# The second layer's first phase as three staggered streams, and the context's recurrence beside the attention

## The chip, the cores and the metric

One core of one Trainium2 chip runs the whole program: TensorE (PE; its weight loads are shown as PEld), VectorE (DVE), ScalarE (ACT), GpSimd (POOL) and SyncE (SP), which issues most of the DMAs. The metric is device time in microseconds for one execution.

## The reference, cut to what matters

Two transformer blocks run one after the other; the first has two layers. The change is in the second of these layers, whose mixer joins a neighbourhood attention to an RWKV-7 recurrence. The recurrence runs in both directions, first over the 256 context tokens from a zero state, then over the 512 latent tokens from the state that the context left:

```python
def odd_mixer(h, hc, ...):
    q, k, v, zd = _split(h @ w_in, (C_W, C_W, C_W, D_SHIFT_W))
    qc, kc, vc, zdc = _split(hc @ w_in, (C_W, C_W, C_W, D_SHIFT_W))
    y_c = neighborhood_attention(heads(q, C_HEADS), heads(k, C_HEADS), heads(v, C_HEADS), kc, vc, rpb)
    lat = rwkv7_inputs(centred_shift_mix(zd, mu), ...)
    cx = rwkv7_inputs(centred_shift_mix(zdc, mu), ...)
    s_fwd, yc_fwd = wkv7_scan(zero, cx, 0, False, need_ctx)
    s_bwd, yc_bwd = wkv7_scan(zero, cx, 1, True, need_ctx)
    _, y_fwd = wkv7_scan(s_fwd, lat, 0, False, True)
    _, y_bwd = wkv7_scan(s_bwd, lat, 1, True, True)
    y_d = rwkv7_readout(y_fwd + y_bwd, lat, r_k, ln_w, ln_b)
    y = jnp.concatenate([y_c, y_d], axis=-1) @ w_out

def step(S, inp):                      # of wkv7_scan
    w_t, k_t, v_t, kk_t, a_t = inp[:5]
    sa = jnp.einsum('bhvk,bhk->bhv', S, kk_t)
    S = (S * w_t[:, :, None, :] - sa[..., None] * (kk_t * a_t)[:, :, None, :]
         + v_t[..., None] * k_t[:, :, None, :])
    return S, (jnp.einsum('bhvk,bhk->bhv', S, inp[5]) if emit else None)
```

There are eight heads of 64 channels. All arithmetic is float32.

## The kernel before

The recurrence is worked in chunks of 64 tokens, and two heads (a pair, `j` from 0 to 3) share the 128 partitions. "c" names the context's stream (4 chunks), "l" the latents' (8 chunks). For each stream the work is cut into three parts.

Phase 1 (`rw_phase1`, `rw_pair`, `rw_dir`) makes everything that doesn't need the state. `mix` makes one projection of 128 channels: 24 matmuls into a PSUM tile `psz`, a shift by POOL (`ms`, L869) and two steps on DVE (L870, L871). There are nine of them in the context's stream and fourteen in the latents'. For each pair and direction `d`, `rw_dir` makes gates and decays from two small products (`psw`, `psa`), a scan and two exponentials on ACT, scales the operands (`az`, `BKn`), multiplies them chunk by chunk into the PSUM tile `psA` (L1004), masks these into `M` on DVE (L1006), makes a second product from `M` and the values (L1011) and stores it all in DRAM. `az` holds the two heads of a pair apart by zeros, so that one product of 128 rows gives both heads, side by side. The tiles `t1` to `t3` exist once for each direction.

`rw_tri` loads the small triangular blocks (`Al`) and solves them on DVE: 31 steps of a product into PSUM (`Tl`, L792) and a subtraction (`Zl`, L794), for both directions, interleaved by the scheduler with whatever else DVE has to do. Its results go to the DRAM images `dZ` and `dZT` (L1041), direction 0 by SP's queue and direction 1 by ACT's. Context and latents use the same images.

`rw_phase2` is the recurrence proper: units (`rw_unit`) of one block of two chunks, one direction and two pairs; 8 units for the context and 16 for the latents. A unit loads its operands, makes a chain of products (`p1`, `p2`, `pb`, `pt`, `p3`: L1070 to L1096, all in PSUM tiles of one pool) with a copy or subtraction by ACT or DVE behind each, and then steps twice through the state `G` (`psc`, L1114 and L1123, with `UV`, L1116, and the update of `G`, L1126). `fl` says how many units are open at once: one for the context, three for the latents.

In program order the layer runs thus: the context's phase 1 with the attention's key and value projections (`na_proj`, PSUM tiles `psn`) between its steps; the latents' phase 1 with the context's solve and the context's recurrence between its steps; the attention (`na_attn`, 32 units of a 128-query block and a head) with the latents' solve between its steps; the latents' recurrence; the readout. Work named `side` is advanced by `step` at each `yield` of the main work. Tiles are allotted in this program order, and each engine then executes its own queue strictly in the order that the scheduler left.

Of the kernel before, what the change touches and what calls it, by code (L numbers as in the profile page):

```python
# [766 lines left out]
class K1:  # L767
# [74 lines left out]
    def rw_phase1(self, s):  # L842
# [4 lines left out]
        with ExitStack() as es:  # L847
# [6 lines left out]
            s.ops = {}  # L854
            s.az = [pi.tile([128, s.nar, 2, n], F32, name=f"az{i}") for i in range(2)]
            s.vu = [pi.tile([128, s.nch, 128], F32, name=f"vu{i}") for i in range(2)]
            for z in s.az + s.vu:
                nc.gpsimd.memset(z, 0.0)
# [3 lines left out]
            def mix(w, cidx, dst):  # L862
# [10 lines left out]
            def mixes(j, gap=1):  # L873
                out = []
                for i, tag in enumerate("kvr" if s.lat else "kv"):
                    out.append(tp.tile([128, n], F32, tag=tag, name=tag))
                    mix(self.wget(("1d", 1 + 4 * i + j)), 1 + 4 * i + j, out[-1])
                    for _ in range(gap):
                        yield
                kvr[j] = out  # L880

            kvr = {}
            mix(self.wget(("1d", 0)), 0, s.tw)
            yield
            nc.scalar.activation(s.tw[0:64], s.tw[0:64], AF.Tanh)
            def gate():
                yield
                mix(self.wget(("1d", 13)), 13, self.gsig)
                nc.scalar.activation(self.gsig, self.gsig, AF.Sigmoid)

            yield from mixes(0)
            self.rw_pair(s, 0, pi, tp, *kvr[0])
            for j in range(4):
                gens = [self.rw_dir(s, d, j, tp) for d in range(2)]
                if j < 3:
                    gens.append(self.chained(mixes(j + 1, 2 if s.lat else 1), lambda: self.rw_pair(s, j + 1, pi, tp, *kvr[j + 1])))
                elif s.lat:
                    gens.append(gate())
                op = s.ops[j]
                while gens:  # L900
                    for g in list(gens):
                        if next(g, self) is self:
                            gens.remove(g)
                    yield
                if s.lat:
                    self.rw_bonus(s, j, op)

    def chained(self, gen, last):
        yield from gen
        last()  # L910

    def rw_pair(self, s, j, pi, tp, k, v, r=None):

        nc = self.nc
        n = s.n
        lora = pi.tile([128, 4, 128], F32, tag="lora", name="lora", bufs=2)
        nc.sync.dma_start(lora, self.ap["lora"][:, :2048].rearrange("p (a b c) -> p a b c", a=4, b=4)[:, :, j])
        kk = tp.tile([128, n], F32, tag="kk", name="kk")
        vu = s.vu[j % len(s.vu)]
        s.ops[j] = (lora, k, v, r, kk, vu, {})  # L920
# [8 lines left out]
        nc.vector.tensor_tensor(kk, kk, sq, op=ALU.mult)  # L929
        pt = s.psd("pvt")  # L930
# [4 lines left out]
        nc.sync.dma_start(s.dV[:, j], vu[64:128])  # L935

# [11 lines left out]
    def rw_dir(self, s, d, j, tp):  # L948
# [3 lines left out]
        lora, k, v, r, kk, vu, kds = s.ops[j]  # L952
# [30 lines left out]
        for e in range(2):  # L983
            p = slice(64 * e, 64 * e + 64)
            if s.lat:
# [9 lines left out]
        w = nar * 128  # L995
        per = 512 // w
        mk = self.b(f"mar{d}")[:, :w].unsqueeze(1).to_broadcast([128, per, w])
        hc = max(per, nch // 2)
        for g in range(0, nch, per):
            if g % hc == 0:  # L1000
                M = tp.tile([128, hc, nar, 2, 64], F32, tag=f"M{d}", name="M", bufs=1)
# [4 lines left out]
            nc.vector.tensor_tensor(M[:, g % hc:g % hc + per].rearrange("p c s e t -> p c (s e t)"), ps.rearrange("p (c x) -> p c x", c=per), mk, op=ALU.mult)  # L1006
            yield
            for c in range(g, g + per):
                for e in range(2):
                    o = ((c - g) // 2) * 128 + e * 64  # L1010
                    nc.tensor.matmul(ps[64 * (c % 2):64 * (c % 2) + 64, o:o + 64], M[:, c % hc, 0, e], vu[:, c, e * 64:e * 64 + 64], start=True, stop=True)  # L1011
            nc.scalar.activation(t2[:, g * 64:(g + per) * 64], ps[:, :per * 64], AF.Copy)
            if (g + per) % hc == 0:
                g0 = g + per - hc
                for c in range(2):
                    nc.sync.dma_start(s.dA[d][:, c, g0 // 2:(g0 + hc) // 2, j].rearrange("p b e t -> p b (e t)"), M[0:64, c::2, 0].rearrange("p b e t -> p b (e t)"))
                if s.lat:
                    nc.sync.dma_start(s.dRR[d][:, j, g0:g0 + hc], M[:, :, 1].rearrange("p c e t -> p c (e t)"))
# [312 lines left out]
    def layer1(self):  # L1331
# [48 lines left out]
        for _ in na:  # L1380
            next(tri, None)
# [835 lines left out]
```

## Time and profile before

| | us |
|---|---|
| median of 3 runs | 3802.57 |
| lowest and highest of them | 3797.42, 3802.86 |
| the profiled execution | 3793.68 |
| its span, first to last instruction | 3791.9 |

PE is busy for 3377.0 us (89% of the span), DVE for 1701.5 (45%), POOL for 1402.0 (37%), ACT for 1308.5 (35%). The mean granted clock of TensorE is 0.945 of full speed. These shares are means over stages with different limits. The second layer's mixer lies between about 1134 and 1866 us from the span's start, and in it PE is less busy than elsewhere.

### The profile page before, as it was taken

Reading aid. Unit: us, or ns where it says so; the run is one execution under the profiler, and the core shown is the slowest. Engines: PE = TensorE matmul, PEld = TensorE weight load, DVE = VectorE, ACT = ScalarE, POOL = GpSimd, SP = SyncE. Lnnn points to the kernel's source line nnn. Section 1 sums busy time; section 2 is a strip of 40 time slices with the busy share of each in tenths; the row PEclk is TensorE's granted clock in tenths of the full one; section 3 lists DMA queues with packets and bytes.
Section 4 is the critical chain, followed back from the end, with each engine's and each line's share of the span. In section 5 each row is a group of like instructions: output and inputs, shape, how many; then the busy total and the mean of one; then the engine's idle time right before and its main releaser. Section 6 shows DMA issues by size and latency. Waiting matters only on the chain. (4 is left out here: it accounts for less than half of the span.)

```text
span 3791.9 us, 49466 instructions
## 1 busy us (share of the span) xinstructions
PE 3377.0 (89%) x18772; PEld 2652.6 (70%) x18772; DVE 1701.5 (45%) x3170; ACT 1308.5 (35%) x2263; POOL 1402.0 (37%) x940
## 2 busy tenths in 40 slices
PE   7989989999999768888889989997898698789997
PEld 3679868787878546667768877666777457658885
DVE  4566231111124596574554426447657767431112
ACT  3366231121224433332234432333545323232222
POOL 1453222222223453321335544434544343244442
PEclk9999999999999878999889999998999899999999
DMA  6420243434334434636423433433455668512221
GB/s 230 164 106 7 88 151 117 150 116 141 126 106 129 111 111 140 175 88 204 146 70 124 131 105 95 122 93 99 140 155 155 158 193 247 164 61 95 95 97 65
DMA packets 397757, 480.78 MB, mean 127 GB/s; under 512 B 148432, under 2 KB 288656, under 8 KB 396496
## 3 DMA queue, kind: packets, MB, share of 16 engines
q1 hardware_dynamic: 384976, 476.05, 40.6%
q10 hardware_dynamic: 12544, 1.57, 0.3%
q8 instruction: 149, 2.44, 0.3%
q14 instruction: 88, 0.72, 0.1%
HBM read 391.86 MB, written 85.66 MB: 126 GB/s over the span
## 5 line engine op out<-in xcount | busy, mean ns | idle before, releaser
L322 POOL TENSOR_TENSOR wlo<-wraw,whi 128x1024 fp32r<-128x1024 f32 (+2 forms) x371 | 867.1, 2339 | 1512.7 <-ACT whi L321 1345.3
L321 ACT ACTIVATE whi<-wraw 128x1024 fp32r<-128x1024 f32 (+2 forms) x371 | 380.2, 1026 | 1041.3 <-issue 240.8
L504 DVE TENSOR_TENSOR pu<-pu,sg 128x512 f32<-128x512 f32 x88 | 55.6, 632 | 606.9 <-PE pu L361 554.2
L361 PE MATMUL pd<-hidh,wlo 128*128 128x512 f32 (+1 forms) x704 | 262.0, 372 | 9.2 <-POOL wlo L322 8.9
L361 PE MATMUL pd<-hidh,whi 128*128 128x512 f32 (+1 forms) x704 | 263.4, 374 | 6.1 <-ACT whi L321 3.8
L361 PE MATMUL pd<-hidl,whi 128*128 128x512 f32 (+1 forms) x704 | 260.5, 370 | 0.2 <-DVE hidl L506 0.2
L361 PE MATMUL pg<-hil,whi 128*128 128x512 f32 x528 | 214.3, 406 | 28.8 <-ACT hil L449 15.4
L361 PE MATMUL pg<-hil,wlo 128*128 128x512 f32 x528 | 211.4, 400 | 8.1 <-POOL wlo L322 7.1
L361 PE MATMUL pu<-hil,whi 128*128 128x512 f32 x528 | 209.7, 397 | 5.8 <-ACT whi L321 5.8
L361 PE MATMUL pu<-hil,wlo 128*128 128x512 f32 x528 | 209.2, 396 | 6.0 <-POOL wlo L322 6.0
L361 PE MATMUL pg<-lol,whi 128*128 128x512 f32 x528 | 210.5, 399 | 2.5 <-DVE lol L450 2.4
L361 PE MATMUL pu<-lol,whi 128*128 128x512 f32 x528 | 208.9, 396 | 0.0
L361 PE MATMUL psp<-hil,whi 128*128 128x512 f32 x416 | 174.0, 418 | 25.6 <-DVE yo L1782 11.8
L361 PE MATMUL psp<-lol,whi 128*128 128x512 f32 x416 | 171.0, 411 | 2.9 <-DVE lol L450 2.9
L361 PE MATMUL psp<-hil,wlo 128*128 128x512 f32 x416 | 170.3, 409 | 1.9 <-POOL wlo L322 1.8
L513 DVE SCALAR_TENSOR_TENSOR xT<-pd,mod,xT 128x512 f32<-128x512 f32 x80 | 59.8, 749 | 244.6 <-PE pd L361 244.6
L361 PEld LDWEIGHTS pd<-hidh,whi 128*128 128x128 f32 x704 | 133.3, 189 | 46.8 <-issue 15.1
L361 PEld LDWEIGHTS pd<-hidh,wlo 128*128 128x128 f32 x704 | 133.4, 189 | 39.1 <-POOL wlo L322 15.4
L361 PEld LDWEIGHTS pg<-hil,whi 128*128 128x128 f32 x528 | 101.5, 192 | 71.8 <-ACT hil L449 18.6
L361 PEld LDWEIGHTS pd<-hidl,whi 128*128 128x128 f32 x704 | 133.3, 189 | 24.0 <-issue 0.9
L792 DVE TENSOR_TENSOR Tl<-Al,Zl 64x31 f32<-64x31 f32 (+15 forms) x248 | 145.2, 585 | 4.1
L1574 DVE SCALAR_TENSOR_TENSOR psp<-xpl,vecs,psp 128x512 f32<-128x512 f32 x144 | 107.8, 751 | 84.5 <-ACT psp L1570 58.1
(588 smaller groups left out, 8145.9 us busy)
## 6 DMA issues: line engine op xcount, KB each, us to landing
mraw<-in_wm_dram SPq DMA_DIRECT2D x144, 512.0 KB, 4.3
wraw<-in_w2c_dram SPq DMA_DIRECT2D x72, 512.0 KB, 3.3
wraw<-in_wf0in_dram SPq DMA_DIRECT2D x44, 512.0 KB, 3.6
wraw<-in_wf1in_dram SPq DMA_DIRECT2D x44, 512.0 KB, 3.6
Z<-dZ SPq DMA_DIRECT2D x48, 256.0 KB, 3.8
ZT<-dZT SPq DMA_DIRECT2D x48, 256.0 KB, 4.1
wraw<-in_w1d_dram SPq DMA_DIRECT2D x23, 512.0 KB, 3.9
wraw<-in_wf2g_dram SPq DMA_DIRECT2D x22, 512.0 KB, 3.2
```

Source lines behind the costliest of these rows:

```text
L321: self.nc.scalar.activation(hi[:, :nk], t[:, :nk], AF.Copy)
L322: self.nc.gpsimd.tensor_tensor(lo[:, :nk], t[:, :nk], hi[:, :nk].bitcast(F32), op=ALU.subtract)
L361: nc.tensor.matmul(ps, l, r, start=first and i == 0 and p == 0, stop=last and i == n - 1 and p == 2)
L504: nc.vector.tensor_tensor(u, u, sg[:, :n], op=ALU.mult)
L513: nc.vector.scalar_tensor_tensor(x[:, j], pd[:, :n], gv[:, j:j + 1], x[:, j], op0=ALU.mult, op1=ALU.add)
L792: nc.vector.tensor_tensor(tmp, A[:L, rows, t:t + 1].to_broadcast([L, nr, ncl]), Z[:L, t:t + 1, cols].to_broadcast([L, nr, ncl]), op=ALU.mult)
L1574: nc.vector.scalar_tensor_tensor(pv, xp[:, :, t:t + L], w(t), pv, op0=ALU.mult, op1=ALU.add)
```

## The change

Phase 1 no longer runs the two directions of one pair beside the next pair's projections. Each pair is one stream (`rw_pair`) that makes its own `k`, `v` and `r` and then opens its two directions two steps apart; up to three such streams are open, started six rounds apart (five in the context's). `az` loses its zeros and its second copy: each head's product takes its own 64 rows, into one PSUM tile for each head. The PSUM pool of the latents' phase 1 has five tiles instead of two; the attention's transposes have one instead of two. The projections beside the context's phase 1 advance at every second step. Only the context's solve stays beside the latents' phase 1; the context's recurrence, with one PSUM tile in each of its two pools instead of two, advances twice in each round of the attention. All stores of the solves go by SP's queue.

```diff
-            s.az = [pi.tile([128, s.nar, 2, n], F32, name=f"az{i}") for i in range(2)]
+            s.az = [pi.tile([128, s.nar, n], F32, name=f"az{i}") for i in range(2)]
...
-            yield from mixes(0)
-            self.rw_pair(s, 0, pi, tp, *kvr[0])
-            for j in range(4):
-                gens = [self.rw_dir(s, d, j, tp) for d in range(2)]
-                if j < 3:
-                    gens.append(self.chained(mixes(j + 1, 2 if s.lat else 1), lambda: self.rw_pair(s, j + 1, pi, tp, *kvr[j + 1])))
...
+            yield from self.rounds((self.rw_pair(s, j, pi, tp, mix) for j in range(4)), 3, 6 if s.lat else 5)
...
+        op = (lora, k, v, r, kk, vu, {})
+        for i, _ in enumerate(self.rounds((self.rw_dir(s, d, j, tp, op) for d in range(2)), 2)):
+            if i == 4 and s.lat:
+                self.rw_bonus(s, j, op)
...
-        for e in range(2):
-            p = slice(64 * e, 64 * e + 64)
-            if s.lat:
-                nc.gpsimd.tensor_tensor(ch(az[p, 1, e]), ch(r[p]), E[p, :, i0:i0 + 64], op=ALU.mult)
-                nc.sync.dma_start(s.dR[d][p, j], az[p, 1, e])
-            nc.vector.tensor_tensor(ch(az[p, 0, e]), ch(kk[p]), E[p, :, iprev:iprev + 64], op=ALU.mult)
-            nc.sync.dma_start(s.dAf[d][p, j], az[p, 0, e])
+        if s.lat:
+            nc.gpsimd.tensor_tensor(ch(az[:, 1]), ch(r), E[:, :, i0:i0 + 64], op=ALU.mult)
+            nc.sync.dma_start(s.dR[d][:, j], az[:, 1])
+        nc.vector.tensor_tensor(ch(az[:, 0]), ch(kk), E[:, :, iprev:iprev + 64], op=ALU.mult)
+        nc.sync.dma_start(s.dAf[d][:, j], az[:, 0])
...
-            ps = s.psv("psA")
+            pa = [s.psv("psA") for e in range(2)]
             for c in range(per):
-                nc.tensor.matmul(ps[:, c * w:c * w + w], BKn[:, g + c].rearrange("p s t -> p (s t)"), az[:, :, :, (g + c) * 64:(g + c) * 64 + 64],
-                                 start=True, stop=True)
+                for e in range(2):
+                    p = slice(64 * e, 64 * e + 64)
+                    nc.tensor.matmul(pa[e][:, c * w:c * w + w], BKn[p, g + c].rearrange("p s t -> p (s t)"), az[p, :, (g + c) * 64:(g + c) * 64 + 64],
+                                     start=True, stop=True)
...
-                        (nc.sync, nc.scalar)[d].dma_start(dst[sl, :, sl].rearrange("i u j -> u i j"), z[Lq * p:Lq * p + Lq])
+                        nc.sync.dma_start(dst[sl, :, sl].rearrange("i u j -> u i j"), z[Lq * p:Lq * p + Lq])
...
-            pT = P("npT", 2, space=PSUM, side="right")
+            pT = P("npT", 1, space=PSUM, side="right")
...
-            st_c.side, st_c.bq, st_c.bc, st_c.bl, st_c.bk = "right", 2, 2, 1, 1
+            st_c.side, st_c.bq, st_c.bc, st_c.bl, st_c.bk = "right", 1, 1, 1, 1
...
-            for _ in self.rw_phase1(st_c):
-                self.step()
+            for i, _ in enumerate(self.rw_phase1(st_c)):
+                if i % 2 == 0:
+                    self.step()
...
-        with self.pool(name="psd1c", bufs=2, space=PSUM) as pA, self.pool(name="psd1f", bufs=2, space=PSUM) as pD:
+        with self.pool(name="psd1c", bufs=2, space=PSUM) as pA, self.pool(name="psd1f", bufs=5, space=PSUM) as pD:
...
-            self.side = chain(self.rw_tri(st_c), self.rw_phase2(st_c))
-            for i, _ in enumerate(self.rw_phase1(st_l)):
-                self.step(2 if i > 16 and i % 2 else 1)
+            self.side = self.rw_tri(st_c)
+            for _ in self.rw_phase1(st_l):
+                self.step()
...
-        tri = self.rw_tri(st_l)
+        tri, rec = self.rw_tri(st_l), self.rw_phase2(st_c)
         for _ in na:
             next(tri, None)
+            next(rec, None)
+            next(rec, None)
         run(tri)
+        run(rec)
```

What this makes of the queues shows at the end of the attention. On PE, before, the attention's last transposes and products (`pt`, `po`) are followed by the latents' recurrence (`p` with L1070 and L1076):

```order
L1259 MATMUL ps<-nkz_12786,nq 128x256
L1289 MATMUL po<-ptile,nv 64x128 x8
L1272 MATMUL pt<-consts,p 128x128 x8
L1289 MATMUL po<-ptile,nv 64x128 x8
L1070 MATMUL p_13946<-ZT,U_13923 128x128 x4
L1076 MATMUL p_13952<-Z,V_13951 128x128 x4
L1070 MATMUL p_13977<-ZT,U_13923 128x128 x4
```

In the changed kernel the same place of PE's queue reads as follows (L1258 and L1275 are the attention's transposes and products, L1056 to L1082 a unit's chain, L1100 and L1109 its steps through `G_9342`; the states and `U_12353`, `U_12354` are the context's):

```order
L1275 MATMUL po<-ptile,nv 64x128 x8
L1258 MATMUL pt<-consts,p 128x128 x8
L1275 MATMUL po<-ptile,nv 64x128 x8
L1056 MATMUL p_13013<-ZT,U_12354 128x128 x4
L1062 MATMUL p_13019<-Z,V_13018 128x128 x4
L1068 MATMUL pb<-consts,BK 128x128 x4
L1072 MATMUL pt<-consts,A 128x128 x2
L1079 MATMUL p_13110<-Z_13096,at 64x128 x4
L1082 MATMUL p_13110<-BV,Z_13096 128x64 x4
L1100 MATMUL psc<-G_9342,LU 64x128 x2
L1056 MATMUL p_13221<-ZT,U_12353 128x128 x3
L1109 MATMUL psc<-UV,bk 128x128 x2
```

This is the fourth of the context's eight units. Three of them stand among the attention's products; the other five stand here, behind all of them and ahead of the latents' recurrence, each but for its `p1` and `p2` behind the one before it.

On SP's queue of the changed kernel the stores of the latents' solve (L1027) stand ahead of that fourth unit's loads of `Z` and `ZT` (L1038, L1039), which read the same images; `dno` is the attention's output:

```order
L1224 DMA nv<-dnv_9436 64x384
L315 DMA wraw<-in_w1out_dram 128x1024
L1027 DMA dZ_1507<-Zl 32x32x32 x4
L1027 DMA dZT_1509<-Al 32x32x32 x4
L1027 DMA dZ_1508<-Zl 32x32x32 x4
L1027 DMA dZT_1510<-Al 32x32x32 x4
L1038 DMA Z<-dZ_1508 128x512
L1280 DMA dno_9439<-no 128x512
L1280 DMA dno_9440<-no 128x512
L1039 DMA ZT<-dZT_1510 128x512
```

Sixteen stores now stand in one queue; before, eight stood in SP's and eight in ACT's. So the fourth unit and all later ones can start only when the latents' solve is done and stored.

On DVE's queue of the changed kernel the solve's last step (L792, L794) stands ahead of ten of the attention's 32 row maxima (`nm`, L1247); before, only one maximum stands within the solve's last two steps, and none behind the last. The place in the changed kernel:

```order
L1247 TENSOR_REDUCE nm<-ps 128x1
L792 TENSOR_TENSOR Tl<-Al,Zl 128x31
L1248 TENSOR_SCALAR nm<-nm 128x1
L792 TENSOR_TENSOR Tl<-Al,Zl 128x31
L794 TENSOR_TENSOR Zl<-Zl,Tl 128x31 x2
L1252 RECIPROCAL sm<-sm 128x1
L1247 TENSOR_REDUCE nm<-ps 128x1
L1248 TENSOR_SCALAR nm<-nm 128x1
L1247 TENSOR_REDUCE nm<-ps 128x1
```

What moved is the end of the solve, from the end of the attention to a place with ten units of it to come.

## Rows read from the trace of the kernel before

**Rows 1.** Busy times by stretch: us, engines (instructions), granted clock, DMA share, GB/s

```profile
1134.00:1304.00 170.00, 138.50 (x888) 119.85 (x888) 86.79 (x157) 75.36 (x136) 74.73 (x54) 0.91 0.45 127
1304.00:1577.00 273.00, 210.40 (x1133) 153.92 (x1134) 199.59 (x335) 97.00 (x162) 106.62 (x72) 0.84 0.44 129
1577.00:1592.00 15.00, 12.94 (x70) 9.30 (x69) 3.78 (x10) 3.01 (x5) 8.24 (x9) 1.00 0.82 240
1592.00:1697.00 105.00, 97.65 (x625) 73.16 (x623) 77.78 (x236) 44.25 (x90) 29.98 (x35) 1.00 0.34 93
1697.00:1714.00 17.00, 2.11 (x17) 1.74 (x18) 0.00 (x0) 1.64 (x2) 0.99 (x2) 0.51 0.85 157
1714.00:1866.00 152.00, 135.11 (x1116) 117.98 (x1116) 79.52 (x218) 46.53 (x107) 33.98 (x54) 0.91 0.60 179
```

**Rows 2.** Groups on DVE, 1304 to 1577: busy us, mean ns, idle before

```profile
L1006 DVE TENSOR_TENSOR M<-psA,consts 128x512 f32<-128x512 f32 x32 | 21.8, 684 | 10.6 <-PE psA L1004 10.5
L988 DVE TENSOR_TENSOR az<-kk,E 64x512 f32<-64x512 f32 x16 | 19.2, 1199 | 0.2
...
L870 DVE SCALAR_TENSOR_TENSOR ms<-ms,psz 128x512 f32<-128x512 f32 x12 | 8.2, 680 | 19.9 <-POOL ms L869 19.9
L1126 DVE TENSOR_TENSOR G<-G,psc 64x128 f32<-64x128 f32 x28 | 7.9, 284 | 5.4 <-PE psc L1123 5.1
...
L964 DVE SCALAR_TENSOR_TENSOR t<-t,kk 128x512 f32<-128x512 f32 x8 | 5.9, 732 | 10.0 <-ACT t L961 9.9
L1116 DVE TENSOR_TENSOR UV<-psc,TB 64x256 f32<-64x256 f32 x14 | 5.8, 417 | 9.4 <-PE psc L1114 5.4 <-ACT TB L1100 1.9 <-ACT t L963 1.6
L1079 DVE TENSOR_TENSOR Z<-Z,p 128x512 f32<-128x512 f32 x8 | 5.5, 684 | 2.6 <-PE p L1076 2.5
...
L1097 DVE COPY LU<-p 128x256 f32<-128x256 f32 x7 | 3.0, 425 | 6.6 <-PE p L1096 6.5
```

**Rows 3.** SP's queue at the attention's end: the solve's stores

```profile
1692.56 4.00 SPq L1041 DMA_DIRECT2D dZ<-Zl  x4
1696.66 8.31 SPq L1041 DMA_DIRECT2D dZT<-Al  x4
```

**Rows 4.** ACT at the attention's end: a copy behind its stores

```profile
1706.18 0.60 ACT L1276 ACTIVATE ptile<-pt 128x512 f32<-128x512 f32 x1 [9.46 <-DMA dZT<-Al]
```

**Rows 5.** The solve's instructions alone in that stretch

```profile
1304.00:1577.00 273.00, 53.50 (x124) 4.07 (x2) 0.00 (x0) 0.84 0.44 129
```

**Rows 6.** Timeline while a context's unit runs: start us, us, instructions [idle before]

```profile
1492.23 0.44 PE L1086 MATMUL pt<-consts,A 128*128 128x128 f32 x2
...
1492.71 0.42 DVE L1088 COPY at<-pt 128x256 f32<-128x256 f32 x1
...
1493.62 0.66 PE L1093 MATMUL p<-Z,at 128*64 128x128 f32 x8
...
1494.21 1.10 PE L1096 MATMUL p<-BV,Z 128*128 128x64 f32 x8
...
1495.87 0.78 ACT L1100 ACTIVATE TB<-p 64x256 f32<-64x256 f32 x2 [1.49 <-DVE LU L1097]
...
1495.97 0.65 PE L1114 MATMUL psc<-G,LU 128*64 128x128 f32 x4
...
1497.14 0.60 ACT L1074 ACTIVATE V<-p 128x512 f32<-128x512 f32 x1 [0.48 <-PE p L1070]
...
1497.88 0.61 PE L1123 MATMUL psc<-UV,bk 128*128 128x128 f32 x4
...
1498.33 1.06 PE L1076 MATMUL p<-Z,V 128*128 128x128 f32 x8
```

**Rows 7.** PE in the latents' phase 1: four of the products into `psA`

```profile
1437.01 1.03 PE L1004 MATMUL psA<-az,BKn 128*128 128x256 f32 x4
```

**Rows 8.** PE while the last unit of the latents' recurrence runs alone

```profile
1852.06 1.23 PE L1112 MATMUL psc<-G,LU 128*128 128x128 f32 x4 [0.52 <-DVE LU L1097]
...
1854.89 1.22 PE L1123 MATMUL psc<-UV,bk 128*128 128x128 f32 x4
```

More of the change, by code (lines that the diff above doesn't have):

```diff
@@ L860, in rw_phase1, with mix @@
             zi = [0]
-            def mix(w, cidx, dst):
+            def mix(cidx, dst):
+                w = self.wget(("1d", cidx))
                 ps = s.psm("psz")
@@ L871, in mix @@
                 nc.vector.scalar_tensor_tensor(dst, t, self.v("mu", cidx), ps, op0=ALU.mult, op1=ALU.add)
[L873 to L882, printed above, removed]
@@ L883, in rw_phase1 @@
-            mix(self.wget(("1d", 0)), 0, s.tw)
+            mix(0, s.tw)
             yield
             nc.scalar.activation(s.tw[0:64], s.tw[0:64], AF.Tanh)
[L886 to L889, printed above, removed]
-            yield from mixes(0)
-            self.rw_pair(s, 0, pi, tp, *kvr[0])
-            for j in range(4):
-                gens = [self.rw_dir(s, d, j, tp) for d in range(2)]
-                if j < 3:
-                    gens.append(self.chained(mixes(j + 1, 2 if s.lat else 1), lambda: self.rw_pair(s, j + 1, pi, tp, *kvr[j + 1])))
[L897 to L904, printed above, removed]
-                if s.lat:
-                    self.rw_bonus(s, j, op)
@@ L908, in chained, with rw_pair @@
[L908 to L912, printed above, removed]
+            yield from self.rounds((self.rw_pair(s, j, pi, tp, mix) for j in range(4)), 3, 6 if s.lat else 5)
+    def rw_pair(self, s, j, pi, tp, mix):
         nc = self.nc
         n = s.n
+        T = lambda tag: tp.tile([128, n], F32, tag=tag, name=tag)
+        k = T("k")
+        mix(1 + j, k)
+        yield
         lora = pi.tile([128, 4, 128], F32, tag="lora", name="lora", bufs=2)
@@ L917, in rw_pair @@
         nc.sync.dma_start(lora, self.ap["lora"][:, :2048].rearrange("p (a b c) -> p a b c", a=4, b=4)[:, :, j])
-        kk = tp.tile([128, n], F32, tag="kk", name="kk")
-        vu = s.vu[j % len(s.vu)]
-        s.ops[j] = (lora, k, v, r, kk, vu, {})
+        kk = T("kk")
         nc.gpsimd.tensor_scalar(kk, k, self.v("k_k", j), 1.0, op0=ALU.mult, op1=ALU.mult)
@@ L929, in rw_pair @@
         nc.vector.tensor_tensor(kk, kk, sq, op=ALU.mult)
+        yield
+        v = T("v")
+        mix(5 + j, v)
+        yield
+        vu = s.vu[j % 2]
         pt = s.psd("pvt")
@@ L935, in rw_pair @@
         nc.sync.dma_start(s.dV[:, j], vu[64:128])
+        r = None
+        if s.lat:
+            yield
+            r = T("r")
+            mix(9 + j, r)
+        yield
+        op = (lora, k, v, r, kk, vu, {})
+        for i, _ in enumerate(self.rounds((self.rw_dir(s, d, j, tp, op) for d in range(2)), 2)):
+            if i == 4 and s.lat:
+                self.rw_bonus(s, j, op)
+            if i == 5 and s.lat and j == 3:
+                mix(13, self.gsig)
+                nc.scalar.activation(self.gsig, self.gsig, AF.Sigmoid)
+            yield
     def rw_bonus(self, s, j, op):
@@ L1022, in rw_dir @@
                 nc.sync.dma_start(s.dBK[d][:, j], BK)
-            yield
+            if g + per < nch:
+                yield
         nc.sync.dma_start(s.dBV[d][:, j].rearrange("p b v -> p (b v)"), t2)
```

37 lines of the change are left out of this document (17 added, 20 removed).

## The prediction

> **What bounds the kernel now.** I read the busy time by stretch first, then the groups on DVE in the stretch that the change rewrites, then the timeline of one context unit, last the queues where the attention ends. The change touches four stretches, and each has another limit [rows 1].
>
> In the context's phase 1 and the junction behind it (1134 to 1304) PE is busy for 138.5 of 170 us and DVE for half: PE sets the pace. In the latents' phase 1 (1304 to 1577) it is the other way round: of 273 us PE is busy for 210.4, at a granted clock of 0.84, and DVE for 199.6. Neither is full; DVE's idle 73.4 us are where it waits for a chain that comes through another engine. The groups show which: the recurrence's own four kinds of step wait 5.4 + 9.4 + 2.6 + 6.6 = 24.0 us, the shift mix waits 19.9 for POOL's `ms`, the masks `M` 10.6 for `psA`, the step `t` 10.0 for ACT [rows 2]. The attention (1592 to 1697) is PE's: 97.65 of 105 us at full clock. From 1697 to 1714 PE has 2.1 us of work [rows 1]: SP stores the solve's result for 4.0 and 8.3 us [rows 3], while ACT, which issues the other half of those stores, reaches the attention's last copy only after 9.46 us of waiting [rows 4]. The latents' recurrence then takes 152 us, with PE busy for 135.1 [rows 1].
>
> **The change part by part.**
>
> *The recurrence leaves the latents' phase 1.* On DVE that removes 7.9 (`G`) + 5.8 (`UV`) + 5.5 (`Z`) + 3.0 (`LU`) us [rows 2] and eight copies `at` of 0.42 [rows 6], 25.6 in all, and the 24.0 us of waits. On PE it removes eight units. One unit is `p1` and `p2` of 1.06, `pb` (four of the transposes of which `pt` has two at 0.44; estimate 0.60), `pt` 0.44, `p3` about 1.7, two `psc` of 0.65 and two updates of 0.61 [rows 6]: 7.4 us, so 59 for eight. The context's solve stays (53.5 us of DVE [rows 5]).
>
> *`az` without zeros.* The two half-width products on DVE become one: 16 instructions of 1199 ns [rows 2] become 8 of 128 partitions and the same 512 columns. The nearest rows give one of them 684 to 1199 ns; I take the upper, so 9.6 us go. The masks stay 32 instructions of 512 columns (two heads by four chunks, where it was four head-chunk pairs), so their 21.8 us stay [rows 2]. POOL and SP lose half of their `az` work and DMAs, in that stage no bound.
>
> *Compact products.* Where PE made four products of 256 columns for each group of four chunks (eight instructions; four of them 1.03 us [rows 7], so 2.06), it makes eight of 128 columns with half the rows, sixteen instructions. The 64-row form stands nowhere in this trace. Its bounds: eight full instructions of 128 columns took 1.06 (`p2`), and eight that each use one half of PE's columns 0.66 [rows 6]; so a group is 1.32 to 2.12, and the sixteen latent groups save 12 us of PE or cost 1. PE has 210.4 − 59 = 151 us left there, below DVE's demand, so I count neither. In the context's phase 1 a group was eight instructions of 128 columns, 1.06, and becomes sixteen of 64 columns, 1.32 to 2.20 (eight such took 1.10 [rows 6]): eight groups cost 2 to 9 us of PE. PE sets the pace there, but is idle for 31.5 of the 170 us, and DVE's `az` halves; I take 0 (0 to 9).
>
> *Three streams and five PSUM tiles.* DVE's demand in the stretch becomes 199.6 − 25.6 − 9.6 = 164.4 us. Its idle time without the recurrence's waits is 73.4 − 24.0 = 49.4. How much of this stays cannot be read: below, 9 us (waits of about 5% of its work, where always another stream is ready); above, the old 73. The waits on POOL's `ms` and on `psA` are the kinds that a second stream covers, but `t1` to `t3` still exist once for each direction, so the third stream stops at the gates of the first. I take 28, somewhat more than half of the 49. The stretch becomes 164 + 28 = 192 in place of 273: **−81** (−100 to −35).
>
> *The lead-in* (1577 to 1592, DVE busy 3.8 of 15 [rows 1]): the last context unit and the pool change behind it no longer lie there: **−6** (−8 to 0).
>
> *The attention* gets three of the eight units: 3 × 7.4 = 22 us on PE, which is full there [rows 1]. Waits come on top, since a unit's next product stands in PE's queue among the attention's and waits for `V1` or `at` behind the solve on DVE (77.8 of 105 us busy), and the transposes have one PSUM tile, so that each waits for ACT's 0.60 us copy [rows 4]: I add 6. **+28** (22 to 40).
>
> *The gap* behind it: the solve now ends ten attention units before the attention's end (10 × 105/32 = 33 us). Its sixteen stores by SP alone take 2 × (4.0 + 8.3) = 24.6 us [rows 3], less than 33, and ACT has none. The 17 us go: **−17**. Should the cover fail, up to 10 come back.
>
> *Five units with nothing beside them.* The fourth unit's loads of `Z` and `ZT` stand behind the latent solve's stores on SP, so it and four more run after the attention. One PSUM tile serves `p1` to `p3`, so a unit's `p1` waits for the copies of the unit before. From one `LU` to the next: `LU` 0.42 and `Z` 0.68 [rows 2]; `TB` 0.78, `p1` and `p2` 2.1, `V1` and `bk` 0.60 each, `pb` 0.60, `pt` 0.44, `at` 0.42, `p3` 1.7 [rows 6]: 8.3. The handoffs lie between 0.04 (`pt` to `at`) and 0.49 us (`at` to `p3`) [rows 6]; five of each kind make 2.6. So 10.9 us a unit. With some 8 to the first `LU` and 6 for the last unit's two steps: 8 + 4 × 10.9 + 6 = 58 at full clock. At half clock PE's part doubles: four products last 1.22 to 1.23 us where the update of the same form lasted 0.61 [rows 6, 8], so 4.9 us more a unit and 2.5 for the last steps: 58 + 27 = 85, with longer waits 91. PE would be busy for 7.4 of 10.9 us, 68%. The nearest stretches are the latents' phase 1 (77% busy, 0.84) and the latents' last unit alone, which fell to half [rows 1, 8]. I take the middle: **+70** (57 to 91).
>
> *The latents' recurrence*: its first loads wait for less, since the solve has long been stored: **−4** (−10 to 0).
>
> Sum: −81 − 6 + 28 − 17 + 70 − 4 = −10 us. The durations are those of the profiled execution (3793.7), which is 9 us below the median of the three runs (3802.6); the stretches bear the difference evenly, so the sum goes to the median: 3792.
>
> **A rule against it.** The product of L1096 begins 0.59 us after that of L1093 began, which takes 0.66: no gap, though one uses half of PE's columns and the other all [rows 6]; going by that row, the alternation of 64-row and 128-row products costs nothing. The Trainium skill ("TensorEngine Tiling (Array Packing)", Key Properties) says the opposite: a change of the tiling mode, not only of the tile, drains TensorE. By that rule the sum would be some 24 us worse, as rival 4 works out; no row here shows the 64-row mode.
>
> **The rivals.**
>
> 1. *The tail at half clock* (0.23, slower). The five serial units leave PE idle for a third of the time; rows 8 speak for the fall, rows 1 against, since all stretches of 77% or more keep 0.84 and above. The tail becomes 85 to 91, the attention grows by 35 to 40: net +12 to +23, and +36 where phase 1 takes 205 as well (its upper end under the forecast). It decides from a tail of some 80 us: the gain elsewhere is then used up. 3815 to 3839.
>
> 2. *Phase 1 comes down to DVE's demand* (0.20, faster). The three streams cover nearly all of DVE's waits, the stretch is 164 + 9 = 173, or 165 if one `az` product costs 684 ns and not 1199 (8 × 0.5 = 4 us) and PE's halves overlap: net −29 to −65. For it: 30 of the 49 us of waits are for POOL and `psA`, which five tiles and other streams relieve. Against: the single `t` tiles. 3738 to 3770.
>
> 3. *Phase 1 does not do what its streams should* (0.06, slower). The streams stop at the single `t1` to `t3` and DVE's idle stays 73: 164 + 73 = 237, only −36. Net +35: 3838.
>
> 4. *Each change between compact and full products empties PE* (0.04, slower). 24 groups of compact products, two changes each, sixteen of them in the latents' phase 1; at the 0.52 us of a handoff to PE [rows 8] the 48 changes of both streams are 25 us. That takes the waits for `psA` from 10.6 [rows 2] upward by as much, where DVE has no other stream ready: net +14, 3816.
>
> **How the numbers follow.** The forecast has 0.47, with its own range from 3765 to 3812 (phase 1 by ±15, tail by ±12, attention by ±6). About 0.2%, 7.6 us, can be told from no change. Of the 0.47, 0.27 are faster, 0.13 within, 0.07 slower. Rival 1 gives 0.21 slower and 0.02 within, rival 2 0.20 faster, rivals 3 and 4 0.10 slower: faster 0.47, same 0.15, slower 0.38. The range reaches into rivals 1 and 2: 3745 to 3840.
>
> **What would show each step.** In the profile of the changed kernel: the latents' phase 1 at 175 to 210 us with DVE busy for about 164 and its waits for `ms` and `psA` below 20 together; `az` as 8 instructions of 0.7 to 1.2 us; the attention at 127 to 145 us, with three context units in it; no stretch of 10 us without PE work behind it but five units with a period near 11 us (near 16 at half clock), `p1` waiting for `TB`'s copy; SP's sixteen stores within the attention; the latents' recurrence at 142 to 152 us. The prediction is wrong if the tail passes 80 us, if the solve does not end ahead of the attention's last ten units in time as it does in order, or if the streams wait for each other's `t` tiles.

## The result: 1.0% slower, and the profile after

The changed kernel took 3837.5 us (median of 4 runs, 3834.9 to 3844.5) against 3802.0 for the kernel before: a ratio of 1.0104 (95% interval 1.0087 to 1.0120). The profiled execution took 3834.9, 41 us more than that of before. 3792 was forecast; the time lies inside the range's upper end, 3840, but on the other side of no change.

In the changed kernel the five later context units read the images after the latents' solve has stored there, so that part of the recurrence works on other numbers. This changes no instruction, and the times are read as they stand; images of the context's own, in the first experiment, take that away.

Busy times by stretch of the changed kernel, columns as in [rows 1] (us, PE, PEld, DVE, ACT, POOL, granted clock, DMA share, GB/s); the stretches are the context's phase 1, the latents' phase 1, the lead-in, the attention, the five units with the ramp of the latents' recurrence, and that recurrence:

```profile
1134.00:1307.00 173.00, 145.02 (x965) 122.27 (x964) 81.69 (x160) 77.06 (x140) 69.03 (x50) 0.92 0.43 122
1307.00:1532.00 225.00, 158.84 (x866) 111.17 (x866) 159.83 (x263) 82.33 (x118) 87.30 (x53) 0.79 0.39 119
1532.00:1538.00 6.00, 5.39 (x24) 4.13 (x22) 0.00 (x0) 0.72 (x2) 1.06 (x3) 1.00 0.90 259
1538.00:1676.00 138.00, 122.51 (x810) 92.87 (x810) 90.48 (x263) 51.41 (x106) 36.03 (x42) 0.98 0.50 125
1676.00:1770.00 94.00, 64.99 (x343) 53.41 (x344) 20.04 (x50) 13.43 (x26) 7.08 (x12) 0.69 0.40 124
1770.00:1902.00 132.00, 119.23 (x1039) 105.15 (x1038) 74.16 (x201) 42.26 (x100) 31.54 (x50) 0.95 0.55 161
```

The reader sees a phase 1 of 225 us in which neither PE (159) nor DVE (160) is full, and a stretch of 94 us, new, at a granted clock of 0.69. Between fixed points of both traces (first and last instruction of a kind) the layer's mixer grew from 734.0 to 771.6 us:

| | before | after | change | forecast |
|---|---|---|---|---|
| context's phase 1, to `k` of the first latent pair | 178.3 | 178.2 | 0 | 0 |
| latents' phase 1, to its last product | 271.4 | 225.1 | −46 | −81 |
| lead-in, to the attention's first product | 17.0 | 6.3 | −11 | −6 |
| attention (before: up to the gap at 1697) | 104.7 | 137.7 | +33 | +28 |
| the gap of stores | 17 | 0 | −17 | −17 |
| five units, to the last product of their state | 0 | 73.5 | +74 | +70 |
| ramp to the latents' first state product | 16.6 | 21.2 | +5 | −4 |
| latents' recurrence | 129.1 | 129.6 | 0 | 0 |

One row stands out: phase 1 gave 35 us less than forecast, of 48 missed in all.

The latents' phase 1 in three pieces (ramp, up to the end of the context's solve, behind it):

```profile
1307.00:1331.00 24.00, 21.44 (x85) 15.91 (x86) 8.46 (x13) 9.08 (x12) 8.53 (x6) 0.92 0.27 87
1331.00:1441.00 110.00, 77.89 (x435) 53.87 (x434) 100.94 (x196) 42.41 (x64) 40.98 (x24) 0.83 0.38 120
1441.00:1532.00 91.00, 59.51 (x350) 41.39 (x348) 50.44 (x56) 30.83 (x43) 37.79 (x24) 0.72 0.43 125
```

While the solve lasts DVE is busy for 92% of the time; in the 91 us behind it for 55%. The groups on DVE over the whole stretch (mean ns, idle before) answer to [rows 2]:

```profile
L992 DVE TENSOR_TENSOR M<-psA,consts 128x512 f32<-128x512 f32 x32 | 21.1, 678 | 8.2 <-PE psA L989 5.6 <-DMA rwl<-M 2.6
...
L870 DVE SCALAR_TENSOR_TENSOR ms<-ms,psz 128x512 f32<-128x512 f32 x12 | 8.1, 678 | 30.3 <-POOL ms L869 30.3
...
L951 DVE SCALAR_TENSOR_TENSOR t<-t,kk 128x512 f32<-128x512 f32 x8 | 7.1, 893 | 7.9 <-ACT t L948 7.9
...
L973 DVE TENSOR_TENSOR az<-kk,E 128x512 f32<-128x512 f32 x8 | 6.8, 855 | 0.0
```

The waits for `M` and `t` are less, that for POOL's `ms` is 30.3 us where it was 19.9. Half of it is one wait, in DVE's timeline, for the last pair's `r`:

```profile
1468.95 0.68 DVE L932 TENSOR_TENSOR kd<-psb,v 128x512 f32<-128x512 f32 x1
1484.25 0.69 DVE L870 SCALAR_TENSOR_TENSOR ms<-ms,psz 128x512 f32<-128x512 f32 x1 [14.62 <-POOL ms L869]
1484.97 0.75 DVE L871 SCALAR_TENSOR_TENSOR r<-ms,vecs,psz 128x512 f32<-128x512 f32 x1
```

The third pair isn't done in this wait: its last four masks stand behind this mix on DVE. PE does not rest either. It is busy without a break with the third pair's products and the matmuls of this mix, at a granted clock of 0.50, the lower of its two levels (1.2 of 2.4 GHz):

```profile
1469.30:1478.00 8.70, 8.70 (x40) 6.48 (x39) 0.33 (x1) 1.18 (x2) 0.00 (x0) 0.50 0.37 105
...
1491.58 2.48 DVE L992 TENSOR_TENSOR M<-psA,consts 128x512 f32<-128x512 f32 x4
```

From 1499 on the fourth pair is alone. Then DVE waits at the links of its chain, for 6.3 us at ACT's `t` and for 3.5 at `psA`.

Behind the attention the `LU` copies of the five units show their period:

```profile
1691.76 0.42 DVE L1083 COPY LU<-p 128x256 f32<-128x256 f32 x1 [3.12 <-PE p L1082]
1704.81 0.42 DVE L1083 COPY LU<-p 128x256 f32<-128x256 f32 x1 [2.47 <-PE p L1082]
...
1743.87 0.42 DVE L1083 COPY LU<-p 128x256 f32<-128x256 f32 x1 [3.12 <-PE p L1082]
```

It is (1743.87 − 1691.76) / 4 = 13.0 us, between the 10.9 of full clock and the 16 of half. SP's queue at the attention's end (answering to [rows 3]) shows the solve's sixteen stores done in 14.4 us, before the attention ends, and what the fourth unit's `ZT` stands behind:

```profile
1644.38 2.54 SPq L1027 DMA_DIRECT2D dZ<-Zl  x4
...
1655.16 3.58 SPq L1027 DMA_DIRECT2D dZT<-Al  x4
1658.92 0.64 SPq L1038 DMA_DIRECT2D Z<-dZ  x1
1659.60 17.55 SPq L1280 DMA_DIRECT2D dno<-no  x2
1677.31 0.32 SPq L1039 DMA_DIRECT2D ZT<-dZT  x1
```

The stores of the attention's own output (`dno`), which wait for its last product, stand between `Z` and `ZT` and hold the queue for 17.55 us. The order printed with the change shows that place; the prediction read only the solve's stores in it.

### The profile page after: what moved, and what is told of

Read it like the earlier page. It is cut to its first block, busy times and chain, and to the rows that moved or that the text cites. A ratio compares the mean times of both kernels' runs of the same rounds, so it can differ in the third digit from the quotient of the medians.

```text
span 3833.1 us, 49756 instructions
## 1 busy us (share of the span) xinstructions
PE 3405.9 (89%) x18964; PEld 2671.1 (70%) x18964; DVE 1684.5 (44%) x3162; ACT 1306.2 (34%) x2248; POOL 1379.9 (36%) x928
## 5 line engine op out<-in xcount | busy, mean ns | idle before, releaser
L361 PEld LDWEIGHTS pg<-hil,whi 128*128 128x128 f32 x528 | 101.5, 192 | 71.8 <-ACT hil L449 19.2
L792 DVE TENSOR_TENSOR Tl<-Al,Zl 64x31 f32<-64x31 f32 (+15 forms) x248 | 142.6, 575 | 4.4
```

The lines of the kernel that those rows point to most:

```text
L361: nc.tensor.matmul(ps, l, r, start=first and i == 0 and p == 0, stop=last and i == n - 1 and p == 2)
L792: nc.vector.tensor_tensor(tmp, A[:L, rows, t:t + 1].to_broadcast([L, nr, ncl]), Z[:L, t:t + 1, cols].to_broadcast([L, nr, ncl]), op=ALU.mult)
```

## The experiments

Each kernel is the changed one with the edit shown, unless said otherwise; `...` stands where lines of an edit are left out. The ratio is to the kernel before, on the same chip.

**The later units' place.** Own images for the context:

```diff
+        self.dZc, self.dZTc = ([self.tc.dram_tile([128, 16, 128], F32, name=f"{n}{d}") for d in range(2)] for n in ("dZc", "dZTc"))
...
-        s.dZ, s.dZT = (... for zz in (self.dZ, self.dZT))
+        s.dZ, s.dZT = (... for zz in ((self.dZ, self.dZT) if s.lat else (self.dZc, self.dZTc)))
```

> The changed kernel with images dZ and dZT of the context's own, so that no load of a context unit stands behind the latents' stores. In the changed kernel five units run alone behind the attention, 73 us longer between the attention's last product and the latents' first state product than before, 14.6 a unit. If the shared images are what puts them there, all but one or two units move beside the attention, where the first three cost 32.6 us, 10.9 a unit: 4 x (14.6 - 10.9) = 15 us less, and up to 25 if the tail's half-clock work goes too: 3812 to 3823. If the units are serial by their own chain and merely change place, the time stays within 8 us of 3837.5.

Measured: 3808.4 us, ratio 1.0019 (1.0006 to 1.0031): 29 us less than the changed kernel, more than the 15 to 25 expected. The attention, then what lies up to the latents' first state product:

```profile
1539.00:1691.00 152.00, 141.70 (x980) 111.06 (x980) 97.78 (x290) 57.69 (x117) 40.08 (x48) 0.98 0.55 135
1691.00:1738.00 47.00, 32.03 (x182) 26.83 (x180) 9.80 (x24) 7.99 (x15) 3.38 (x6) 0.72 0.65 188
```

Most units now lie beside the attention: it grew by 15 us, and what follows shrank by 48. So a unit costs less there than the 10.9 us taken from the first three, whose 32.6 us must hold more than the units themselves. The shared images were what put the five units there.

**The recurrence back beside phase 1.**

```diff
...
-            self.side = self.rw_tri(st_c)
-            for _ in self.rw_phase1(st_l):
-                self.step()
+            self.side = chain(self.rw_tri(st_c), self.rw_phase2(st_c))
+            for i, _ in enumerate(self.rw_phase1(st_l)):
+                self.step(2 if i > 16 and i % 2 else 1)
...
```

The lines left out take the recurrence away from the attention and give the streams four PSUM tiles.

> The changed kernel with the context's recurrence back beside the latents' phase 1 (four PSUM tiles for its streams, not five, since the recurrence needs two). Theory: the latents' phase 1 fell by 46 us only because its last 60 us, one pair alone, have nothing beside them on DVE; then the recurrence fits there and the stretch grows from 225 to 240 to 262 us, the attention falls from 138 to 105, the units behind it go, and the gap of stores behind the attention comes back with 17 to 25 us: 3837 - 73 - 33 + 25 + 20 = 3776 (3765 to 3792). Rival: the three streams stop each other at their single t tiles and gain nothing by themselves; then the stretch is 273 again and the time 3800 to 3815.

Measured: 3807.4 us, ratio 1.0016 (1.0007 to 1.0026), the rival's time but not its reason. Phase 1 and lead-in:

```profile
1305.00:1552.00 247.00, 188.89 (x1065) 136.26 (x1065) 169.38 (x293) 86.46 (x130) 87.03 (x55) 0.80 0.41 123
1552.00:1616.00 64.00, 52.65 (x280) 41.42 (x278) 16.25 (x43) 10.44 (x21) 13.09 (x17) 0.76 0.48 126
```

Phase 1 is within the 240 to 262, but the units run on alone for most of 64 us behind it. The next kernel paced them (two steps a round, three in every fourth):

```diff
-                self.step(2 if i > 16 and i % 2 else 1)
+                self.step(2 if i % 4 else 3)
```

> The run before it with the recurrence beside phase 1 left 33 of the side work's 74 steps to the lead-in, since phase 1 now has 33 rounds where it had 52. Here the side work advances two and three steps a round and ends with phase 1. If only that pace was wrong, phase 1 and lead-in together fall from 311 us to 250 to 275: 3758 (3746 to 3772). If the units can't lie beside the streams (single t tiles, one PSUM tile each), the two stay near 300: 3795 or more.

Measured: 3805.3 us, ratio 1.0014 (1.0002 to 1.0025). Its second case came: phase 1 is 274 us, as long as before the change, with lead-in 290, where the first case had 250 to 275. Up to 1440, while the solve lasts, and behind it:

```profile
1308.00:1440.00 132.00, 99.07 (x511) 69.30 (x512) 107.57 (x203) 50.37 (x74) 49.81 (x29) 0.82 0.37 116
1440.00:1583.00 143.00, 115.35 (x747) 88.03 (x746) 74.76 (x124) 44.98 (x73) 43.37 (x35) 0.84 0.50 143
```

The units begin only when the solve is done, so all eight meet the last pair, and two serial chains share PE's and DVE's queues: 143 us with DVE 52% and PE 81% busy. So work that fits by its sum on DVE doesn't fit here. That the two chains are the reason, rather than PE, is argued, not shown.

**The solve's pace.** One step of the solve at every fourth round of phase 1 (`if i % 4 == 3: self.step()`):

> The changed kernel with the context's solve advanced at every fourth step of the latents' phase 1 instead of every one, so that its 53 us of DVE reach to the last pair. If DVE is the bound between 1331 and 1469 (91% busy) and the last pair's idle is only lack of other work, the stretch falls by 12 to 20 us: 3818 to 3826. If the streams' own chain sets the pace, it stays: 3832 to 3843. The recurrence's first units may start later, since the context's solve is stored later: up to 10 us more behind the attention.

Measured: 3814.9 us, ratio 1.0038 (1.0025 to 1.0051), 22.6 less than the changed kernel and more than the 12 to 20 expected. Behind the ramp, and then the lead-in:

```profile
1328.00:1500.00 172.00, 126.86 (x794) 90.15 (x793) 133.61 (x238) 65.40 (x100) 86.79 (x46) 0.84 0.46 145
1500.00:1521.00 21.00, 10.30 (x34) 7.46 (x32) 3.68 (x18) 5.35 (x4) 6.11 (x6) 0.66 0.72 147
```

Phase 1 took 194 us, where 225 had been and 192 was forecast; 15 came back in the lead-in. DVE's busy time fell with it, from 160 to 145 us for the same instructions. So of the 31 us that phase 1 lost, 19 are work of DVE (15 by shorter instructions, 4 by steps of the solve that moved into the lead-in), and only 12 are waiting. The last pair's `r` is written at 1463.8, 159 us into the phase; in the changed kernel at 1485.0, 178 us in.

**The t tiles.**

```diff
-        T = lambda i: tp.tile([128, n], F32, tag=f"t{i}{d}", name=f"t{i}", bufs=1)
+        T = lambda i: tp.tile([128, n], F32, tag=f"t{i}{d}", name=f"t{i}", bufs=2)
```

The three kernels with this edit give other values than the rest, and why isn't settled. The instructions and their sizes are the same, so their times are read, but none of them can take the place of the kernel before.

> The changed kernel with two of each of the tiles t1, t2 and t3 for a direction instead of one. If the streams wait for each other at these tiles (the rival of the prediction in which phase 1 gives only 36 us), the phase falls from 225 to 195 to 210 us: 3807 to 3823. If the last pair's lack of other work is the cause, it stays within 8 us: 3830 to 3845.

Measured: 3824.8 us, ratio 1.0074 (1.0060 to 1.0089): 12.7 less, between the two cases. Phase 1 took 204.7 us, as the first case has it, the lead-in 11.5. So the single t tiles held the streams back as well, and `r` of the last pair comes 164 us into the phase. With the solve spread (below) the second tile adds nothing to phase 1.

**Compact products.** `az` with its zeros and products of 128 rows, in the streams' own steps:

```diff
...
-                for e in range(2):
-                    p = slice(64 * e, 64 * e + 64)
-                    nc.tensor.matmul(pa[e][:, c * w:c * w + w], BKn[p, g + c]..., az[p, :, ...], start=True, stop=True)
+                nc.tensor.matmul(pa[c // sub][:, i * w:i * w + w], BKn[:, g + c]..., az[:, :, :, ...], start=True, stop=True)
...
```

> The changed kernel with az's zeros and the products of 128 rows back, all else as changed (the same steps and PSUM tiles in the streams). If a change between products of 64 and of 128 rows empties TensorE, this kernel is faster, by up to 25 us (3812). In the changed kernel's profile sixteen compact instructions take 1.16 to 1.23 us at full clock, so I expect no such cost: DVE gets 8 x 0.9 + some 5 us of work back, PE 10 to 13: slower by 0 to 15 us, 3838 to 3853.

Measured: 3850.0 us, ratio 1.0127 (1.0111 to 1.0143), 12.5 slower than the changed kernel, as expected. Phase 1 took 235 us:

```profile
1310.00:1545.00 235.00, 154.82 (x739) 109.41 (x740) 171.26 (x271) 81.63 (x117) 100.12 (x60) 0.82 0.41 115
...
L975 DVE TENSOR_TENSOR az<-kk,E 64x512 f32<-64x512 f32 x16 | 17.8, 1115 | 0.2
```

It is 10 us longer than in the changed kernel, and DVE has 171 us of work in it in place of 160. Those 11 us are `az`, whose sixteen half-width instructions came back with the zeros. PE is busy for 155 us, no more than the 159 of the changed kernel. So this run prices the smaller `az` and the compact products together; what the products are worth by themselves it doesn't show. In the changed kernel, PE's timeline shows the compact products next to full ones:

```profile
1455.44 1.12 PE L893 MATMUL psk<-sqk,consts 128*128 128x512 f32 x2 [0.19 <-ACT sqk L891]
1456.49 1.16 PE L989 MATMUL psA<-az,BKn 64*128 64x128 f32 x16
...
1463.15 0.48 PE L998 MATMUL psA<-vu,M 128*64 128x64 f32 x2 [0.70 <-DVE M L992]
1463.56 1.23 PE L989 MATMUL psA<-az,BKn 64*128 64x128 f32 x8
```

L989 begins at 1456.49, within L893's 1.12 us, and at 1463.56 within L998's 0.48, so PE isn't seen empty there. But the profile models the ends of PE's instructions, and the starts of single instructions in the trace show a price. At full clock, full products of 128 columns begin 0.11 us apart, also where one line's products follow another's (L1076 to L1082 before the change). Between the last compact instruction and the first of another shape, 0.20 us pass, and the second one behind it is often 0.1 us late as well. So a change of shape costs 0.1 to 0.2 us. The kernel before pays it too, wherever products of 64 and of 128 columns meet: 94 times in the latents' phase 1. In the changed kernel there are 69 such changes, 46 of them to or from 64 rows.

Sixteen compact instructions, the heads in turn, take 1.16 us at full clock, less than the 1.32 that the prediction had as its lower bound. The 1.23 us of the last line, which the expectation takes for another measurement of this, are eight instructions at a granted clock of 0.50.

**PSUM tiles.** Three instead of five in the streams' pool (`bufs=3`):

> The changed kernel with three PSUM tiles, not five, in the pool of the latents' phase 1. If the tiles are what brought the stretch from 271 to 225 us, 20 to 46 us come back: 3857 to 3884. If the streams' order did (two tiles are taken by each group of products, and DVE waits only 8 us for psA), 0 to 10: 3837 to 3848.

Measured: 3851.5 us, ratio 1.0134 (1.0121 to 1.0147): 14 slower, between the two. Phase 1 took 243 us, so two of the five tiles are worth 18 of the 46 that it fell, and DVE's wait for `psA` doubled to 16.2 us.

**Together.** Own images, the solve at every third round, three steps of the recurrence in each round of the attention:

```diff
...
+            for i, _ in enumerate(self.rw_phase1(st_l)):
+                if i % 3 == 2:
+                    self.step()
...
+            for _ in range(3):
+                next(rec, None)
```

> The changed kernel with the context's own images, the context's solve advanced at every third round of phase 1 (it then ends with it), and the recurrence advanced three times, not twice, in each round of the attention, so that all eight units lie beside the attention. Against the kernel with images alone (3808) phase 1 with lead-in should fall from 232 us to 200 to 210, as it did with the slower solve (194 and 21), and the attention with what lies behind it by 5 to 15: 3773 (3763 to 3785). If a later solve only delays the units, nothing is left of the first part: 3795 to 3805.

Measured: 3774.9 us, ratio 0.9928 (0.9915 to 0.9940), faster than both kernels, and the time is as expected. Phase 1 took 196 us, the lead-in 20 (together 215, where 200 to 210 was expected), the attention 167 with all eight units, and 23 follow to the first state product of the latents. The lead-in is long because the solve's stores now end on SP just ahead of the attention's loads:

```profile
1508.17 1.63 SPq L1029 DMA_DIRECT2D dZc<-Zl  x3
...
1515.06 2.52 SPq L1029 DMA_DIRECT2D dZTc<-Al  x4
...
1521.00 1.14 SPq L1222 DMA_DIRECT2D nkz<-dnk  x2
```

So the solve was advanced in two of five rounds (`if i % 5 in (0, 2)`):

> The kernel with the context's own images, paced solve and three steps of the recurrence (3774.9), with the solve advanced in two of five rounds, so that it ends six rounds ahead of phase 1. There the solve's sixteen stores stood on SP ahead of the attention's loads and the lead-in was 19.8 us (6.3 in the changed kernel). If those stores are the cause, the lead-in falls to 6 to 9 and phase 1 grows by 0 to 8, since the last pair loses some cover: 3763 to 3775. If the lead-in stays at 18 or more, the loads themselves are late: 3775 to 3783.

Measured: 3777.1 us, ratio 0.9948 (0.9933 to 0.9963). The lead-in fell to 8.2 us and phase 1 stayed at 197, as expected, but the time is above the 3763 to 3775 that went with it and not below the kernel ahead of it: the stages of its profiled execution sum to 702 us against 714, yet that execution was the fastest of its six (3762) and the other's the slowest of its five (3787). Whether the 12 us are kept is open. With two of each t tile added:

> The kernel with the context's own images, three steps a round and the solve advanced in two of five rounds (3777.1), with two of each t tile. If the t tiles cost nothing, 3770 to 3783; if they do in the evenly loaded phase, where DVE still waits 50 of 195 us, the phase falls by 5 to 20 more: 3757 to 3772.

Measured: 3765.9 us, ratio 0.9910 (0.9895 to 0.9926). Phase 1 stayed at 199 us, so the lower time, which is in the second case's range, has not come from where the second tile works. Where it came from is open.

**What the streams are worth.** The kernel before, with its old phase 1, and the recurrence beside the attention as in the kernel of 3774.9. The solve is advanced at every fourth of its 52 rounds, and the solves' stores still go by two queues:

> The kernel before (its phase 1 with one pair's two directions beside the next pair's projections, and full products), but with the recurrence beside the attention as in the kernel of 3774.9: own images, solve paced over phase 1, three steps a round, five PSUM tiles. Its phase 1 is 52 rounds long. It tells what the streams are worth by themselves. If most of the shorter phase 1 is only the recurrence's leaving (25.6 us of work and 24 of waits, less what the last pair lacks), phase 1 is 215 to 230 us and the time 3795 to 3810; if the streams are worth little, 200 and 3780; if they are worth all, 250 or more and 3825.

Measured: 3803.5 us, ratio 1.0013 (1.0002 to 1.0024); phase 1 took 222.7 us, within the first case's 215 to 230. And the streams with full products:

> The last kernel (own images, paced solve, three steps a round, two of each t tile; 3765.9) with az's zeros and the products of 128 rows back. Against the kernel with the old phase 1 and the recurrence beside the attention (3803.5) it has the streams and nothing of the compact products. If compact products are worth what they were in the changed kernel (12.5 us), 3774 to 3784, and the streams alone are worth 20 to 30; if the compact products carry most of the gain over the old phase 1, 3790 to 3803.

Measured: 3799.4 us, ratio 1.0002 (0.9988 to 1.0016). Phase 1 took 214 us. The time is the second case's. It misses the first case by 15 us: 14 of these lie behind the attention, where 37 us follow and not 23, because the last unit and the end of the one ahead of it came to stand behind the attention's last product. Phase 1 of the three kernels, with the old order, with streams and full products, and with streams and compact products (the kernel of 3765.9):

```profile
1309.00:1532.00 223.00, 152.59 (x737) 107.34 (x738) 173.53 (x272) 83.81 (x134) 103.57 (x60) 0.80 0.42 119
1309.00:1523.00 214.00, 155.77 (x734) 109.55 (x736) 175.23 (x271) 79.55 (x116) 102.50 (x60) 0.83 0.42 122
1308.00:1507.00 199.00, 147.38 (x866) 104.40 (x867) 155.98 (x263) 80.02 (x117) 90.78 (x52) 0.84 0.43 133
```

So the old phase 1 is 223 us without the recurrence, and the streams bring 8. Those 8 are not of the streams alone, since that kernel also has the second t tile, another pace of the solve and one queue for its stores. Compact products with the smaller `az`, all else alike, bring 16 more, and DVE's work falls by 19 with them.

## Why the prediction was wrong

**The step that failed** is the one on the three streams: of DVE's 49 us of idle time "I take 28, somewhat more than half". DVE's demand was right, 164 forecast and 160 measured. Its idle time was 65 (225 − 160). A run agrees with the 49 too: the old phase 1 without the recurrence leaves DVE idle for 223 − 174 = 49 us. What was wrong is how much of it the streams would cover. Where the solve is spread over phase 1, they leave 39 to 53 us (43 in the kernel of 3765.9), and no run comes near 28. In the changed kernel they cover nothing, and 16 us of waiting come on top. The prediction's own sign for this step, waits for `ms` and `psA` below 20 us together, reads 36 (30.3 and 5.6).

Two edits bring most of this back, each by itself. One is to the solve's place. The prediction subtracted work and waits from a stretch as if what is left were spread over it. The order has the solve advance at every round, and phase 1 now has 33 rounds where it had 52, so its 53 us of DVE lie in the first 134 us. Behind the ramp DVE is 92% busy in these and holds the streams back, and in the 91 us behind them, with the end of the third pair and then the fourth pair alone, 55%. In the slower solve nothing else changed, and phase 1 took 194 us: the solve's place costs 31 us. The other edit is the second t tile, which took 20 us off.

The forecast of 192 would be nearly reached by the kernel with the slower solve, but not by the sum that gave it. In it DVE has 142 us of work and 53 of idle: less work than the 164, more waiting than the 28. DVE is then not the bound; PE is at 76%, DVE at 73%. That the streams' chain sets the pace there is argued.

**Rival 3** (phase 1 gives 36 us, 3838) named the time nearly exactly, which is luck in part: phase 1 and lead-in came out 15 us better than it has them, the attention, the units and the ramp 18 worse. Its reason is half right, as the t tiles show. Both cures start the last pair sooner (its `r` 159 and 164 us into the phase, not 178), and either alone takes 20 to 31 us; together they take no more than one. A late and lonely last pair would fit these runs, but it isn't shown to be the path: with full products and with three PSUM tiles `r` comes at 169 and 170 us, and phase 1 is longer (235 and 243). Which path the two cures share stays open.

**The recurrence's leaving** was sized well. With the old phase 1 and the recurrence elsewhere the stretch fell from 271 to 223, by 49 us; the sum had 25.6 of work and 24.0 of waits. (That kernel also has five PSUM tiles and another pace of the solve.) Put back beside the streams at a paced step, with one PSUM tile fewer, it took phase 1 back up by 49.

**The five units** were right in place and size: 73.5 us forecast as 70, at a granted clock of 0.60 to 0.81. Rival 1 (85 to 91 at half clock) did not come. The ramp behind them was 5 us more where 4 less was forecast: the latents' first loads go out only at 1750.4, behind the context's last step, and from there to the first state product it takes 20 us, as before the change (from 1710.9). The own images removed 29 us, which bears out that the shared images are the cause; the attention's output on the same queue holds `ZT` back for the 17.55 us seen there, but PE's order has the units behind the attention anyway.

**The attention** was 33 longer against 28, within its 22 to 40; **the gap** of stores went, as forecast; its stores took 14.4 us, not 24.6.

**Rival 4** (changes between compact and full products empty PE) had its price too high: 0.1 to 0.2 us a change, not 0.52, and fewer changes in the latents' phase 1 than before. But the prediction's reading of [rows 6], that the alternation costs nothing, was wrong too. From the last start of L1093 to the first of L1096 0.20 us pass, where the starts within either line are 0.11 apart (those of L1093 in pairs). So the rule of the Trainium skill's page "TensorEngine Tiling (Array Packing)", Key Properties, that a change of the tiling mode drains TensorE, agrees with the trace. The same section's second property, that tiles work independently, agrees with the 16 instructions in 1.16 us: the two heads' products begin in pairs, one pair each 0.11 us.

**Rival 2**'s figures give a net of −29 to −37; what takes it on to −65, and so to 3738, it doesn't say.

**`az`** took 855 ns an instruction, not 1199. So 16 instructions of 19.2 us became 8 of 6.8: 12.4 saved, 9.6 forecast.

## What to carry to other kernels

A stretch's idle time belongs to a place in it: before one subtracts it, one should see where it lies, and where the filler work ends once the rounds that pace it grow fewer. Streams that are started one after another leave the last one alone, and filler that reached to it took 31 us off the stretch here. When a unit of work is moved, the buffers that it shares with the next piece of work in program order decide whether it can really go where the code puts it.

## What the hardware showed unexpectedly

DVE's instructions with two SBUF inputs change in length from kernel to kernel, and those that read PSUM don't. `az` took 1199 ns before (64 partitions, [rows 2]) and 855 in the changed kernel (128 partitions); in the kernel with the slower solve:

```profile
L992 DVE TENSOR_TENSOR M<-psA,consts 128x512 f32<-128x512 f32 x32 | 21.1, 680 | 11.6 <-PE psA L989 9.7 <-DMA rwl<-M 1.8
...
L870 DVE SCALAR_TENSOR_TENSOR ms<-ms,psz 128x512 f32<-128x512 f32 x12 | 8.2, 685 | 28.7 <-POOL ms L869 28.7
...
L973 DVE TENSOR_TENSOR az<-kk,E 128x512 f32<-128x512 f32 x8 | 5.4, 675 | 0.0
```

`M` and `ms`, with one input in PSUM, stay at 678 to 685 ns in all three, while `az` falls to 675. The Trainium skill ("SBUF — State Buffer", Who interferes with whom) says that such DVE instructions contend with GpSimd's reads for a shared port. The trace of before agrees: 15 of its 16 `az` lie over POOL's work and take 1232 ns in the mean, the other one took 690. Overlap alone doesn't decide, though: with the slower solve six of eight lie over POOL's work and take 675. With the slower solve DVE's work for the same instructions fell from 160 to 145 us. A duration taken from a crowded stretch is thus not that of the same instruction in another one.
